# A decoder layer on one core: the first heads' keys and queries as a block pair by seven products, and a fourth such quad in the mixer

## The chip, the core and the metric

The kernel runs on one core of a Trainium2 chip. TensorE multiplies matrices into PSUM banks, VectorE (DVE), ScalarE (ACT) and GpSimd (POOL) work on elements, and the DMA queues move data. Each engine has a queue of its own and takes its instructions in order; semaphores tie the queues together. The metric is the device time of one execution in microseconds (us), lower is better.

## The reference

The layer works on 256 tokens of 2048 features, in float32. One norm feeds one projection, whose columns are queries, keys and values of eight heads and the input of a pooling mixer. Heads and mixer are joined, projected and added to x; then comes a gated feed-forward part with a convolution of width 3.

```python
h = rms_norm(x, attn_norm_g[l])
proj = h @ w_in[l]                       # 2048 x 4096: q, k, v, p of 1024 columns each
q = rms_norm(heads(q), q_norm_g[l]);  k = rms_norm(heads(k), k_norm_g[l])   # per head of 128
a = moba_attention(q, k, heads(v), rel_bias)      # 256 tokens: one causal block
m = multiscale_pool(p, pool_w[l], pool_scale[l])  # windows 2, 4, 8, 16
x = x + jnp.concatenate([a, m], axis=-1) @ w_out[l]
x = x + conv_ffn(rms_norm(x, ffn_norm_g[l]), w_up[l], conv_w[l], conv_b[l], w_down[l])
```

## The kernel before

**Precision.** Every float32 operand of a large product is held as two parts, high and low, in a type that TensorE reads in one pass. A product is three matmuls: high by high, low by high, high by low. Activations are split once. Weights come from memory as float32 and are split on the way: ScalarE copies the high part `wh` (`split_high`, line 142), VectorE subtracts it from the raw weights to get the low part `wl` (`split_low`, line 147).

**Steps.** All weights are one stream of chunks of 128 x 2048, each of two units of 128 x 1024. There are as many steps as units, in the list `steps`; step u is the products of unit u. A half step of plain products is 12 matmuls with 512 columns. The order of the work is written out by hand in the loop at the end of `layer`: in its turn u it emits the high part of unit u + 6, the low part of unit u + 5, the products of unit u, and then whatever `after(u, f)` has hung on that step. So each engine's queue is in the order of this loop. There are four buffers for raw chunks (the next chunk is loaded when one is released), seven for `wh` and six for `wl`.

**Stages before the feed-forward part.** Steps 0 to 15 make the values v of all heads. Steps 16 to 31 make keys and then queries of the first four heads, steps 32 to 47 those of the second four, each as a `tok_block` of eight half steps that accumulates into two PSUM banks, and ends in `head_norm`: ScalarE squares, VectorE reduces, the reciprocal root is taken, VectorE scales. `head_T` turns the result with TensorE; `scores`, `normalise`, `probs_T` and `head_out` are the attention of one head, spread over the steps of the next stage. Steps 48 to 63 are the pooling input. Steps 64 to 81 multiply by the first 1024 columns of the output weights (and by the pooling weights, in between). Steps 82 to 97, the "mixer's block pair", multiply by the other 1024 columns.

**Block pairs and quads.** `down_pair` makes 256 tokens by 1024 columns with four banks, in eight quads (six in the last third of the feed-forward part) of two units. A quad is two feature tiles by two halves of the tokens by two halves of the columns: eight block products, 24 matmuls (`quad`, line 790). Some quads, listed in `MIXED` and `OUT_MIXED`, go by seven products instead (Winograd's form of Strassen's scheme), 21 matmuls (`quad_sums`, line 734). They need sums of blocks of both operands:

- of the weights: `seven_sums` (lines 161 to 163) makes three differences in the raw chunk, and these are split too, into `wh`/`wl` and the tiles `s512` and `s1024`, of which there are two sets (`SECOND` says which quads take the second);
- of the activations: `token_sums` (line 721) makes four sums of 128 tokens on GpSimd, and ScalarE and VectorE split them into `sx` (lines 722, 723).

The first product goes to the bank `aux[0]`, the second to `p5`, the third to `p7`, the fourth to `aux[1]`; three more go straight to the four banks of the pair. `p5` and `p7` are the two small banks, which are also used by the row sums, the scores and the transposes of the probabilities. `add_part` adds `aux`, `p5` and `p7` later.

In the mixer three quads go by seven products (the fourth, sixth and seventh); `mixed_sums` makes their token sums in steps 72 to 77.

**Norm of the input.** The gain is applied to x when it is split, the root mean square later. ScalarE squares x (`square`), GpSimd adds the squares up (`add_squares`, line 357), TensorE sums over partitions and `stats1` (lines 363 to 373), hung on step 18, makes what the heads and the pooling need. The row sum is read from a small bank.

Of the kernel before, what the change touches and what calls it, by code (L numbers as in the profile page):

```python
# [25 lines left out]
F32 = mybir.dt.float32  # L26
# [5 lines left out]
P = 128  # L32
# [28 lines left out]
OUT_MIXED = (3, 5, 6)  # L61
OUT_SECOND = (5,)
# [23 lines left out]
def layer(ctx: ExitStack, tc: tile.TileContext, xT, xtok, wts, par, rel_d, ident_d, icnt_d, out):  # L86
# [261 lines left out]

    def square(a):

        n = min(4 * S, G0 - 4 * a * S)
        nc.scalar.activation(xsq[:, a, :n], xboth[:, 4 * a * S:4 * a * S + n], AF.Square)
        if n < 4 * S:
            nc.scalar.activation(xsq[:, a, n:], xin(0), AF.Square)

    def add_squares(a, b, n):
        nc.gpsimd.tensor_tensor(xsq[:, a, :n], xsq[:, a, :n], b, op=OP.add)

    def stats1():
# [3 lines left out]
        nc.tensor.matmul(ps[:, :S], ones, xsq[:, 0, :S], start=True, stop=True)  # L363
# [19 lines left out]
    def head_norm(ps, name):  # L383
# [11 lines left out]
        n = early.tile([P, NT * 4, HD], F32, name=name, tag="hn")  # L395
# [168 lines left out]
    steps += v_blocks()  # L564
    for b in range(2):
        for nm in ("k", "q"):
            st[nm, b, "end"] = len(steps) + 7
            steps += tok_block(lambda: xh, XT, lambda ps, nm=nm, b=b: st.__setitem__((nm, b), head_norm(ps, nm + "n")))
    for g in (3, 2, 1, 0):
        steps += feat_block(lambda: xh, lambda ps, g=g: pool_window(ps, g))  # L570
        after(len(steps) + (2 if g else 0), lambda g=g: pool_mixed(g))

    assert AHEAD not in PAIRS
    for a, u in enumerate((2, 4, 7, 10)):
        after(u, lambda a=a: square(a))
# [4 lines left out]
    after(10, load_consts)  # L580
    after(18, stats1)
    after(15, load_late)
    after(17, bias_rows)
    after(24, lambda: st.__setitem__(("T", 0), bias_tile(0)))
    for b in range(2):
        for nm, gc in (("k", col(C_KG)), ("q", qs)):
            after(st[nm, b, "end"] + (3 if (nm, b) == ("q", 0) else 2), lambda nm=nm, b=b, gc=gc: st.__setitem__(
                (nm + "T", b), head_T(st[nm, b], gc, nm + "T")))
        at = st["q", b, "end"] + (3 if b else 4)
        for j in range(4):  # L590
            h, u = 4 * b + j, at + 2 * j
# [20 lines left out]

    def open_late():
# [5 lines left out]
        late["sx"] = pool.tile([P, 4, 4, 2, P], F32R, name="sx")  # L619
# [81 lines left out]
    def value(ps, g, j):  # L701
# [7 lines left out]
        if j in late["mixed"]:  # L709
            token_sums(y, j)  # L710

    def token_sums(y, i):
# [3 lines left out]
        sx = late["sx"]  # L716
        s = late["pool"].tile([P, 4, P], F32, name="s", tag="s")
        a11, a21, a12, a22 = y[:, 0, :P], y[:, 0, P:], y[:, 1, :P], y[:, 1, P:]
        for n, (a, b, op) in enumerate(((a21, a22, OP.add), (s[:, 0, :], a11, OP.subtract), (a11, a21, OP.subtract),
                                        (a12, s[:, 1, :], OP.subtract))):  # L720
            nc.gpsimd.tensor_tensor(s[:, n, :], a, b, op=op)  # L721
        nc.scalar.activation(sx[:, i, :, 0, :], s, AF.Copy)
        nc.vector.tensor_tensor(sx[:, i, :, 1, :], s, sx[:, i, :, 0, :].bitcast(F32), op=OP.subtract)

    def mixed_sums(k, i):
# [3 lines left out]
        token_sums(y, i)  # L729
# [6 lines left out]
    def down_pair(bp, nq, final, mixer=False):  # L736
# [4 lines left out]
        order = [2 * k for k in ORDER[nq]]  # L741
        if mixer:
            mixed, second, summed, order = OUT_MIXED, OUT_SECOND, OUT_MIXED, OUT_ORDER
        s_end = 2 * mixed[-1] + 1
        rest = 2 * nq - 1 - s_end

        def hid(k, t):
            act = st["cat"] if mixer else late["hid"]
            return [act[:, k, a, t * P:(t + 1) * P] for a in range(2)]

        def sums(i, n):
            return [late["sx"][:, i, n, a, :] for a in range(2)]
# [118 lines left out]
        for j in range(nq):  # L871
            for h in range(2):
# [12 lines left out]
                for i, n in enumerate((4, 0, 1) if apart else range(5)):  # L885
                    if at == s_end + 1 + (i * (rest - 1) // 5 if end else 0):
                        acts.append(lambda n=n: add_part(n))
# [6 lines left out]
        return runs  # L894

# [11 lines left out]
    steps += down_pair(1, 8, False, True)  # L907
# [58 lines left out]
def chunks(w_in, pool_w, w_out, w_up, w_down):  # L966
# [6 lines left out]

    out = []
    for tiles in V_TILES:
        out.append(np.concatenate([w_in[k * P:(k + 1) * P, 2048 + 512 * b:2560 + 512 * b] for k, b in tiles], axis=1))
    for c0 in (1024, 0, 1536, 512):
# [7 lines left out]

    def halves(w, c0, ks):
        both = []
        for k in ks:
            top, low = (w[i * P:(i + 1) * P, c0:c0 + 1024] for i in (k, k + 1))
# [48 lines left out]
```

## Time and profile before

| | |
|---|---|
| time, median of 3 runs | 1012.52 us (1012.18 to 1013.14) |
| profiled execution, its own time | 1012.62 us |
| span of the profiled execution | 1010.8 us, 13627 instructions |
| TensorE busy (matmul / weight load) | 1006.6 us / 865.0 us |
| VectorE, ScalarE, GpSimd busy | 812.9, 571.4, 92.6 us |
| read from memory | 195.83 MB, 196 GB/s over the span |

The span runs from the first to the last instruction of the profiled execution; its time is 1.8 us more. A busy TensorE means that a matmul was under way. In the groups and timelines a row names the line, the engine, the operation, what it writes and reads, and the shapes; in brackets stands the idle time before it and what ended it. In the chain of waits each row is a stretch of the chain that ended last: start, duration, engine, tile, line and count.

### The profile page before, as it was taken

Reading aid. Unit: us, or ns where it says so; the run is one execution under the profiler, and the core shown is the slowest. Engines: PE = TensorE matmul, PEld = TensorE weight load, DVE = VectorE, ACT = ScalarE, POOL = GpSimd, SP = SyncE. Lnnn points to the kernel's source line nnn. Section 1 sums busy time; section 2 is a strip of 40 time slices with the busy share of each in tenths; the row PEclk is TensorE's granted clock in tenths of the full one; section 3 lists DMA queues with packets and bytes.
Section 4 is the critical chain, followed back from the end, with each engine's and each line's share of the span. In section 5 each row is a group of like instructions: output and inputs, shape, how many; then the busy total and the mean of one; then the engine's idle time right before and its main releaser. Section 6 shows DMA issues by size and latency. Waiting matters only on the chain.

```text
span 1010.8 us, 13627 instructions
## 1 busy us (share of the span) xinstructions
PE 1006.6 (100%) x5250; PEld 865.0 (86%) x5250; DVE 812.9 (80%) x1021; ACT 571.4 (57%) x773; POOL 92.6 (9%) x125
## 2 busy tenths in 40 slices
PE   9999999999999999999999999999999999999998
PEld 8888888888888888888888888888888888888887
DVE  6956666886986888878999678887899977887897
ACT  6744464555565655655566456565555655565572
POOL 0520004601000000000000010000000000000010
PEclk9999999999999999999999999999999999999999
DMA  9784454475453554644676645555357775545474
GB/s 345 275 279 167 167 188 167 168 289 179 166 216 108 187 217 179 240 176 167 231 227 239 220 167 177 214 198 211 140 192 219 290 239 180 191 167 200 175 229 147
DMA packets 32481, 205.49 MB, mean 203 GB/s; under 512 B 3784, under 2 KB 4680, under 8 KB 9632
## 3 DMA queue, kind: packets, MB, share of 16 engines
q1 hardware_dynamic: 29680, 195.84, 52.8%
q0 software_dynamic: 2736, 8.78, 4.3%
q8 instruction: 41, 0.67, 0.3%
q14 instruction: 24, 0.20, 0.1%
HBM read 195.83 MB, written 2.49 MB: 196 GB/s over the span
## 4 chain that ended last, share of the span: by engine, by line
PE 100%; DVE 0%; issue 0%
PE ps_feat L203 35%; PE ps_feat L205 18%; PE ps_down L790 16%; PE ps_tok L190 13%; PE ps_p L734 6%; PE ps_down L734 4%; PE ps_v L197 4%; PE ps_pool L212 1%; PE ps_s L418 1%; PE ps_start L265 0%; PE ps_down L812 0%; PE ps_T L405 0%; PE ps_x2T L651 0%; PE ps_av L451 0%; PE ps_eT L440 0%; PE ps_av L452 0%
## 5 line engine op out<-in xcount | busy, mean ns | idle before, releaser
L203 PE MATMUL ps_feat<-x2h,wh 128*128 128x512 f32 x1408 | 488.9, 392 | 0.0
L147 DVE TENSOR_TENSOR wl<-raw,wh 128x1024 fp32r<-128x1024 f32 x358 | 433.6, 1252 | 42.1 <-ACT wh L142 19.5
L142 ACT ACTIVATE wh<-raw 128x1024 fp32r<-128x1024 f32 x358 | 358.6, 1049 | 104.6 <-DVE raw L161 68.9
L205 PE MATMUL ps_feat<-x2h,wl 128*128 128x256 f32 x1408 | 393.6, 280 | 0.0
L203 PEld LDWEIGHTS ps_feat<-x2h,wh 128*128 128x128 f32 x1408 | 264.3, 188 | 58.2
L205 PEld LDWEIGHTS ps_feat<-x2h,wl 128*128 128x128 f32 x1408 | 264.4, 188 | 0.2
L790 PE MATMUL ps_down<-wh,hid 128*128 128x512 f32 x384 | 94.8, 389 | 0.0
L689 ACT ACTIVATE y<-u,pv 128x256 f32<-128x256 f32 x88 | 48.2, 594 | 77.1 <-DVE u L684 77.1
L790 PEld LDWEIGHTS ps_down<-wh,hid 128*128 128x128 f32 x384 | 72.1, 188 | 15.0
L190 PE MATMUL ps_tok<-wh,xh 128*128 128x512 f32 x256 | 70.1, 396 | 0.0
L690 DVE SCALAR_TENSOR_TENSOR y<-u,pv,y 128x256 f32<-128x256 f32 x88 | 42.4, 482 | 29.5 <-ACT y L689 29.5
L190 PEld LDWEIGHTS ps_tok<-wh,xh 128*128 128x128 f32 x256 | 47.5, 188 | 9.4
L790 PE MATMUL ps_down<-wl,hid 128*128 128x512 f32 x192 | 51.3, 389 | 0.0
L820 POOL DMA_DIRECT2D x<-st x13 | 11.5, 920 | 416.6 <-ACT st L861 282.7
L468 DVE TENSOR_TENSOR fs<-ps_feat,fs 128x512 f32<-128x512 f32 x44 | 30.3, 688 | 21.0 <-ACT fs L467 20.9
L203 PE MATMUL ps_feat<-xh,wh 128*128 128x512 f32 x128 | 46.2, 402 | 0.0
L692 DVE SCALAR_TENSOR_TENSOR y<-u,pv,y 128x256 f32<-128x256 f32 x88 | 42.7, 485 | 3.1
L790 PEld LDWEIGHTS ps_down<-wl,hid 128*128 128x128 f32 x192 | 36.0, 188 | 7.5
L707 ACT ACTIVATE hid<-y 128x512 fp32r<-128x512 f32 x22 | 14.0, 634 | 48.9 <-DVE y L706 48.9
L721 POOL TENSOR_TENSOR s<-y 128x128 f32<-128x128 f32 x22 | 13.7, 624 | 292.7 <-DVE y L706 242.6
L190 PE MATMUL ps_tok<-wl,xh 128*128 128x512 f32 x128 | 39.5, 390 | 0.0
L467 ACT ACTIVATE fs<-ps_feat 128x512 f32<-128x512 f32 x44 | 25.8, 586 | 21.0 <-PE ps_feat L205 20.7
(199 smaller groups left out, 1178.7 us busy)
## 6 DMA issues: line engine op xcount, KB each, us to landing
raw<-in_wts SPq DMA_DIRECT2D x177, 1024.0 KB, 5.0
x<-st POOLq DMA_DIRECT2D x11, 512.0 KB, 10.7
raw<-in_wts SPq DMA_DIRECT2D x4, 512.0 KB, 7.3
x<-in_xtok SPq DMA_DIRECT2D x1, 2048.0 KB, 9.6
raw<-in_wts SPq DMA_DIRECT2D x7, 256.0 KB, 5.5
xboth<-in_xT SPq DMA_DIRECT2D x4, 256.0 KB, 6.1
T<-band POOLq DMA_DIRECT2D x8, 128.0 KB, 7.2
out<-x POOLq DMA_DIRECT2D x2, 512.0 KB, 4.0
```

Source lines behind the costliest of these rows:

```text
L142: nc.scalar.activation(wparts[u][0], raw(u - 1 if u - 1 in seven else u + 1 if u in seven else u), AF.Copy)
L147: nc.vector.tensor_tensor(wl, raw(u - 1 if u - 1 in seven else u + 1 if u in seven else u), wh.bitcast(F32), op=OP.subtract)
L190: nc.tensor.matmul(ps[:, t, :], act[:, k0 + k, a, t * P:(t + 1) * P], w[:, k * 512:(k + 1) * 512], start=(first and k == 0 and n == 0), st ...
L197: nc.tensor.matmul(ps[:, t, :], act[:, k, a, t * P:(t + 1) * P], w[i], start=(first and n == 0), stop=(last and n == 2))
L203: nc.tensor.matmul(ps, wh[:, ws], act[:, k, :, :], start=(first and n == 0), stop=False, skip_group_check=True)
L205: nc.tensor.matmul(ps[:, S:], wl[:, ws], act[:, k, 0, :], start=False, stop=(last and n == len(ks) - 1), skip_group_check=True)
L468: nc.vector.tensor_tensor(dst, ps[:, :, :S], dst, op=OP.add)
L689: nc.scalar.activation(y[:, m, :], u[:, m, 2:], AF.Identity, scale=cw[2], bias=col(C_CB + f))
L690: nc.vector.scalar_tensor_tensor(y[:, m, :], u[:, m, 1:1 + S], cw[1], y[:, m, :], op0=OP.mult, op1=OP.add)
L692: nc.vector.scalar_tensor_tensor(y[:, m, :], u[:, m, :S], cw[0], y[:, m, :], op0=OP.mult, op1=OP.add)
L734: nc.tensor.matmul(ps, act[a], w[i], start=(first and n == 0), stop=(last and n == 2), skip_group_check=skip)
L790: nc.tensor.matmul(bank(t, b), hid(order[j] + h, t)[a], part(w, b if h == 0 else 1 - b)[i], start=(n == 0 and (fresh or mixed[0] == 0 and ...
```

## The change

- **Heads.** Keys and queries of the first four heads become one block pair, `down_pair(0, 8, False, "heads")`, in steps 16 to 31: the left 512 columns are keys, the right 512 queries. The quads at positions 2, 3, 5 and 6 go by seven products (steps 20 to 23 and 26 to 29); the second and the last of these take the second set of tiles. `head_sums` adds the two parts of x, makes the four token sums on VectorE in steps 16, 18, 20 and 22, and `sums_split` splits them two steps later each. One of the pair's two bank pairs comes from `aux`, and its bank pair `ps_p` from the accumulators. `head_parts` (step 30) and `heads_end` (step 31) put the result together in SBUF. `head_norm` of the keys follows at step 31, of the queries at step 32.
- **Attention of the first heads.** The keys are turned at step 34, the queries at step 36; the scores start at step 37 instead of 35. The second keys are turned at step 43 instead of 41.
- **Mixer.** A fourth quad, the third, goes by seven products. Token sums are made on VectorE in steps 70 to 76 and split one step later each. In the feed-forward part they stay on GpSimd.
- **Squares.** They are added on VectorE in steps 5, 8 and 11, the last sum into a tile of its own, `xsum`. `stats1` stays at step 18.
- **Smaller moves.** `bias_rows` goes from step 17 to 24, the first bias tile from 24 to 28, the second from 42 to 44. The weights are laid out for the pair on the host.

```diff
-OUT_MIXED = (3, 5, 6)
-OUT_SECOND = (5,)
+OUT_MIXED = (2, 3, 5, 6)
+OUT_SECOND = (3, 6)
+HEADS_MIXED = (2, 3, 5, 6)
+HEADS_SECOND = (3, 6)
...
     def add_squares(a, b, n):
-        nc.gpsimd.tensor_tensor(xsq[:, a, :n], xsq[:, a, :n], b, op=OP.add)
+        nc.vector.tensor_tensor(xsq[:, a, :n], xsq[:, a, :n], b, op=OP.add)
...
-        nc.tensor.matmul(ps[:, :S], ones, xsq[:, 0, :S], start=True, stop=True)
+        nc.tensor.matmul(ps[:, :S], ones, xsum, start=True, stop=True)
...
+    def open_heads():
+        hs = keep.tile([P, 3 + len(HEADS_MIXED), 1024], F32R, name="hs", tag="c")
+        late["s"] = [seven_tiles(early, 0), [[hs[:, 0, :512], hs[:, 0, 512:]], [hs[:, 1, :], hs[:, 2, :]]]]
+        late["sx"] = [hs[:, 3 + i, :].rearrange("p (n a t) -> p n a t", n=4, a=2)
+                      for i in range(len(HEADS_MIXED))]
...
+    def token_sums(y):
+        eng = nc.gpsimd if "mixed" in late else nc.vector
+        s = late["sums"] = (late["pool"].tile([P, 4, P], F32, name="s", tag="s") if "pool" in late else
+                            early.tile([P, 4, P], F32, name="s", tag="hn"))
         a11, a21, a12, a22 = y[:, 0, :P], y[:, 0, P:], y[:, 1, :P], y[:, 1, P:]
         for n, (a, b, op) in enumerate(((a21, a22, OP.add), (s[:, 0, :], a11, OP.subtract), (a11, a21, OP.subtract),
                                         (a12, s[:, 1, :], OP.subtract))):
-            nc.gpsimd.tensor_tensor(s[:, n, :], a, b, op=op)
-        nc.scalar.activation(sx[:, i, :, 0, :], s, AF.Copy)
-        nc.vector.tensor_tensor(sx[:, i, :, 1, :], s, sx[:, i, :, 0, :].bitcast(F32), op=OP.subtract)
-
-    def mixed_sums(k, i):
+            eng.tensor_tensor(s[:, n, :], a, b, op=op)
+
+    def sums_split(i):
+        sx, s = late["sx"], late["sums"]
+        nc.scalar.activation(sx[i][:, :, 0, :], s, AF.Copy)
+        nc.vector.tensor_tensor(sx[i][:, :, 1, :], s, sx[i][:, :, 0, :].bitcast(F32), op=OP.subtract)
+
+    def head_sums(k):
+        y = early.tile([P, 2, S], F32, name="y", tag="sq")
+        nc.vector.tensor_tensor(y, xh.bitcast(F32)[:, k:k + 2, 0, :], xh.bitcast(F32)[:, k:k + 2, 1, :], op=OP.add)
+        token_sums(y)
...
         def banks():
-            box["tok"] = [acc("ps_down") for t in range(NT)]
+            box["tok"] = [(aux if heads and t == 0 else acc)("ps_down") for t in range(NT)]
...
-                box["aux"], box["p5"], box["p7"] = aux("ps_p"), small("ps_p5"), small("ps_p7")
+                box["aux"], box["p5"], box["p7"] = (acc if heads else aux)("ps_p"), small("ps_p5"), small("ps_p7")
...
+        def head_parts(n):
+            pa_, p5, p7 = box["aux"], box["p5"], box["p7"]
+            if n == 0:
+                box["raw"] = k, q = [early.tile([P, NT, 512], F32, name=t + "raw", tag=t + "T") for t in "kq"]
+                nc.scalar.activation(k[:, 0, :], pa_[:, 0, :], AF.Copy)
+                nc.vector.tensor_tensor(q[:, 0, :], pa_[:, 1, :], k[:, 0, :], op=OP.add)
+                nc.vector.tensor_tensor(k[:, 1, :], p7, q[:, 0, :], op=OP.add)
+            elif n == 1:
+                k, q = box["raw"]
+                nc.vector.tensor_tensor(q[:, 1, :], p5, k[:, 1, :], op=OP.add)
+                nc.vector.tensor_tensor(q[:, 0, :], p5, q[:, 0, :], op=OP.add)
+
+        def heads_end():
+            for b, raw_ in enumerate(box["raw"]):
+                for t in range(NT):
+                    nc.vector.tensor_tensor(raw_[:, t, :], bank(t, b), raw_[:, t, :], op=OP.add)
+            st["k", 0], st["qraw"] = head_norm(box["raw"][0], "kn"), box["raw"][1]
...
+    steps += v_blocks()
+    h0 = len(steps)
+    after(12, open_heads)
+    st["k", 0, "end"] = st["q", 0, "end"] = h0 + 15
+    for i, j in enumerate(HEADS_MIXED):
+        after(h0 + 2 * i + 2, lambda i=i: sums_split(i))
+        after(h0 + 2 * i, lambda j=j: head_sums(2 * j))
+    steps += down_pair(0, 8, False, "heads")
...
-    after(4, lambda: add_squares(0, xsq[:, 1, :], 4 * S))
-    after(7, lambda: add_squares(0, xsq[:, 2, :], 4 * S))
-    after(10, lambda: (add_squares(0, xsq[:, 3, :], 4 * S), add_squares(0, xsq[:, 0, 2 * S:], 2 * S),
-                       add_squares(0, xsq[:, 0, S:2 * S], S)))
+    after(5, lambda: add_squares(0, xsq[:, 1, :], 4 * S))
+    after(8, lambda: add_squares(0, xsq[:, 2, :], 4 * S))
+    after(11, lambda: (add_squares(0, xsq[:, 3, :], 4 * S), add_squares(0, xsq[:, 0, 2 * S:], 2 * S),
+                       nc.vector.tensor_tensor(xsum, xsq[:, 0, :S], xsq[:, 0, S:2 * S], op=OP.add)))
...
     after(18, stats1)
...
-    after(17, bias_rows)
-    after(24, lambda: st.__setitem__(("T", 0), bias_tile(0)))
+    after(24, bias_rows)
+    after(28, lambda: st.__setitem__(("T", 0), bias_tile(0)))
...
-        at = st["q", b, "end"] + (3 if b else 4)
+        at = st["q", b, "end"] + (3 if b else 6)
+        if b == 0:
+            after(at - 5, lambda: st.__setitem__(("q", 0), head_norm(st["qraw"], "qn", keep, "c")))
...
-        after(o0 + 8 + 2 * i, lambda i=i, j=j: mixed_sums(OUT_ORDER[j], i))
+        after(o0 + 6 + 2 * i, lambda j=j: mixed_sums(OUT_ORDER[j]))
+        after(o0 + 7 + 2 * i, lambda i=i: sums_split(i))
```

More of the change, by code (lines that the diff above doesn't have):

```diff
@@ L347, in layer @@
     rrow = keep.tile([P, S], F32, name="rrow", tag="rrow")
+    xsum = early.tile([P, S], F32, name="xsum")
     def square(a):
@@ L394, in head_norm @@
         rsqrt(r, m, NT * 4, early, "h")
[L395 removed]
+        n = pool.tile([P, NT * 4, HD], F32, name=name, tag=tag)
         nc.vector.tensor_tensor(n, psv, r[:, :, None].to_broadcast([P, NT * 4, HD]), op=OP.mult)
@@ L618, in open_late @@
         nc.sync.dma_start(late["x2"], xtok)
-        late["sx"] = pool.tile([P, 4, 4, 2, P], F32R, name="sx")
+        sx = pool.tile([P, 4, 4, 2, P], F32R, name="sx")
+        late["sx"] = [sx[:, i] for i in range(4)]
         late["s"] = [seven_tiles(pool, 0), None]
@@ L741, in down_pair @@
         order = [2 * k for k in ORDER[nq]]
+        mixer, heads = kind == "mixer", kind == "heads"
         if mixer:
             mixed, second, summed, order = OUT_MIXED, OUT_SECOND, OUT_MIXED, OUT_ORDER
+        if heads:
+            mixed, second, summed, order = HEADS_MIXED, HEADS_SECOND, HEADS_MIXED, XT
         s_end = 2 * mixed[-1] + 1
@@ L747, in hid @@
         def hid(k, t):
-            act = st["cat"] if mixer else late["hid"]
+            act = xh if heads else st["cat"] if mixer else late["hid"]
             return [act[:, k, a, t * P:(t + 1) * P] for a in range(2)]
         def sums(i, n):
-            return [late["sx"][:, i, n, a, :] for a in range(2)]
+            return [late["sx"][i][:, n, a, :] for a in range(2)]
         def bank(t, b):
@@ L884, in down_pair @@
                 acts = [run]
-                for i, n in enumerate((4, 0, 1) if apart else range(5)):
+                for i, n in enumerate(range(2) if heads else (4, 0, 1) if apart else range(5)):
                     if at == s_end + 1 + (i * (rest - 1) // 5 if end else 0):
-                        acts.append(lambda n=n: add_part(n))
+                        acts.append(lambda n=n: (head_parts if heads else add_part)(n))
                         run.adds = not end
@@ L904, in layer @@
     for i, j in enumerate(OUT_MIXED):
-        after(o0 + 8 + 2 * i, lambda i=i, j=j: mixed_sums(OUT_ORDER[j], i))
+        after(o0 + 6 + 2 * i, lambda j=j: mixed_sums(OUT_ORDER[j]))
+        after(o0 + 7 + 2 * i, lambda i=i: sums_split(i))
     after(len(steps) - 1, lambda: open_temps(True))
-    steps += down_pair(1, 8, False, True)
+    steps += down_pair(1, 8, False, "mixer")
     f0 = len(steps)
@@ L972, in feat, with halves @@
         return [w[k * P:(k + 4) * P, c0:c0 + 256].reshape(4, P, 256).transpose(1, 0, 2).reshape(P, HALF) for k in ks]
+    def halves(w, c0, ks):
+        both = []
+        for k in ks:
+            top, low = (w[i * P:(i + 1) * P, c0:c0 + 1024] for i in (k, k + 1))
+            both += [top, np.concatenate([low[:, 512:], low[:, :512]], axis=1)]
+        return both
     out = []
@@ L976, in chunks @@
         out.append(np.concatenate([w_in[k * P:(k + 1) * P, 2048 + 512 * b:2560 + 512 * b] for k, b in tiles], axis=1))
-    for c0 in (1024, 0, 1536, 512):
+    out += halves(np.concatenate([w_in[:, 1024:1536], w_in[:, :512]], axis=1), 0, range(0, KT, 2))
+    for c0 in (1536, 512):
         out += tok(w_in, c0, range(0, KT, 2))
@@ L984, in chunks @@
     out += tok(w_out, 512, OK)
[L986 to L989, printed above, removed]
-            both += [top, np.concatenate([low[:, 512:], low[:, :512]], axis=1)]
-        return both
     out += halves(w_out, 1024, OUT_ORDER)
```

66 lines of the change are left out of this document (33 added, 33 removed).

## The prediction

> **What bounds the kernel now.** First comes the page: how busy each engine is, the granted clock and the chain that ended last.
>
> ```profile
> PE 1006.6 (100%) x5250; PEld 865.0 (86%) x5250; DVE 812.9 (80%) x1021; ACT 571.4 (57%) x773; POOL 92.6 (9%) x125
> ...
> PEclk9999999999999999999999999999999999999999
> ...
> PE 100%; DVE 0%; issue 0%
> ```
>
> TensorE is busy through the whole span at the full clock, and the chain is TensorE alone. Second, the view of who waited for whom, for TensorE, has one row:
>
> ```profile
> PE ps_start L265 <- DVE ones L262: 1.1, 1, 1.1
> ```
>
> So after its start TensorE waits for nobody. A product taken away is worth its full duration, and a wait put in costs its full duration, because nothing later can catch it up. Third, the chain in order of time prices the products (start, duration, what):
>
> ```profile
> 49.06 8.16 PE ps_tok L190 x36
> 57.22 0.43 PE ps_row L363 x2
> 264.55 2.72 PE ps_p L734 x12
> 267.27 2.04 PE ps_down L734 x9
> 269.31 5.44 PE ps_down L790 x24
> ```
>
> A matmul of 512 columns takes 8.16/36 = 0.227 us. A half step is 12 of them, 2.72; a quad is 24, 5.44; a quad by seven products is 12 + 9, 4.76.
>
> Fourth, VectorE where four of eight quads go by seven products today, by stages (span, then busy time of PE, PEld, DVE, ACT, POOL):
>
> ```profile
> 510.00:552.00 42.00, 42.00 (x187) 34.79 (x186) 41.24 (x41) 24.99 (x28) 1.83 (x2) 1.00 0.74 250
> ```
>
> There VectorE works 41.24 of 42 us. Two rows show how closely it serves TensorE: the low part of a combination of weights, and the matmul group that first reads this tile.
>
> ```profile
> 511.75 1.22 DVE L175 TENSOR_TENSOR s1024l<-raw,s1024h 128x1024 fp32r<-128x1024 f32 x1
> 513.79 0.62 PE L734 MATMUL ps_p<-s1024h,sx 128*128 128x512 f32 x2
> ```
>
> The tile is ready 0.8 us before its group starts. So four quads of eight fill VectorE, and that stage makes no token sums of its own. The question is whether the first heads' pair, where the sums come on top, still fits.
>
> **What is removed.** The heads' pair has four quads by seven, each 3 products shorter: 4 x 0.68 = 2.72 us. The mixer goes from three to four: 0.68. Together 3.40 us of TensorE, everything else equal.
>
> **What a quad by seven costs VectorE.** One quad of the mixer, from its first low part to the next unit's:
>
> ```profile
> 268.74 1.22 DVE L147 TENSOR_TENSOR wl<-raw,wh 128x1024 fp32r<-128x1024 f32 x1
> 269.87 0.68 DVE L168 TENSOR_TENSOR s512l<-raw,s512h 128x512 fp32r<-128x512 f32 x1
> 270.59 1.22 DVE L161 TENSOR_TENSOR raw<-raw 128x1024 f32<-128x1024 f32 x1
> 271.85 0.69 DVE L162 TENSOR_TENSOR raw<-raw 128x512 f32<-128x512 f32 x1
> 272.57 0.69 DVE L163 TENSOR_TENSOR raw<-raw 128x512 f32<-128x512 f32 x1
> 273.18 1.22 DVE L147 TENSOR_TENSOR wl<-raw,wh 128x1024 fp32r<-128x1024 f32 x1
> 274.47 1.23 DVE L175 TENSOR_TENSOR s1024l<-raw,s1024h 128x1024 fp32r<-128x1024 f32 x1
> 275.62 4.62 DVE L147 TENSOR_TENSOR wl<-raw,wh 128x1024 fp32r<-128x1024 f32 x4
> ```
>
> The first unit takes 273.18 - 268.74 = 4.44, the second 2.44: 6.88 us, against 4.76 of TensorE. The last row prices a plain unit: 4.62/4, about 1.14 back to back.
>
> **What the token sums add.** They lie beside the mixer today:
>
> ```profile
> 221.37 0.69 DVE L728 TENSOR_TENSOR fs<-cat 128x512 f32<-128x512 f32 x1
> 224.68 0.69 DVE L723 TENSOR_TENSOR sx<-s,sx 128x512 fp32r<-128x512 f32 x1 [2.62 <-ACT sx L722]
> 126.52 0.42 DVE L457 TENSOR_TENSOR cat<-ps_av,cat 128x256 fp32r<-128x256 f32 x1 [1.14 <-ACT cat L456]
> 222.14 0.46 POOL L721 TENSOR_TENSOR s<-fs 128x128 f32<-128x128 f32 x1 [14.74 <-DVE fs L728]
> 58.81 0.17 DVE L371 TENSOR_SCALAR e<-t 128x2 f32<-128x2 f32 x1
> ```
>
> No VectorE sum of 128 columns is in the trace. From 512 columns (0.69) and 256 (0.42) the line goes to 0.29 at 128, which I take; the bounds are 0.17 (two columns) and 0.46 (what GpSimd needs). One set of sums is 0.72 + 4 x 0.29 = 1.88, its low half 0.69 more. Four sets in the heads' pair are 10.3 us. In the mixer VectorE stands 2.62 us per set today, waiting for GpSimd and ScalarE; after the change that wait is gone, as the split comes a step later. There 4 x 2.57 = 10.3 replaces 3 x (0.69 + 2.62 + 0.69) = 12.0 us. After quad 3 it waits for TensorE:
>
> ```profile
> 261.92 1.22 DVE L147 TENSOR_TENSOR wl<-raw,wh 128x1024 fp32r<-128x1024 f32 x1 [1.48 <-PE ps_down L790]
> ```
>
> A fourth quad, 6.88 - 2.28 = 4.6 us, fits: at quad 6 the last tile is ready by 275.62 and first read three triples into the quad, at 269.31 + 5.44 + 4.76 + 2.04 = 281.55; the added quad takes at most 4.6 + 0.68 of these 5.9 us. So I count the mixer's 0.68 in full.
>
> **The squares.** GpSimd's sums cost VectorE time while they run:
>
> ```profile
> 28.03 2.67 POOL L357 TENSOR_TENSOR xboth<-xboth 128x1024 f32<-128x1024 f32 x1 [27.05 <-ACT xboth L352]
> 28.93 2.85 DVE L147 TENSOR_TENSOR wl<-raw,wh 128x1024 fp32r<-128x1024 f32 x1 [0.50 <-ACT wh L142]
> ```
>
> A 1.22 us subtraction takes 2.85 beside one. On VectorE the sums are 3 x 1.23 + 0.69 + 0.42 = 4.8 us in steps 5 to 11, and the stretching goes. I cost this at nothing: VectorE still comes to step 15 ahead of its free tile. If that cover were gone, the start below would move by up to 4.8.
>
> **VectorE's queue through the heads' pair.** It works in the order of the program. The start is set by the low parts' six buffers: unit 20's needs unit 14's. The rule shows here, where the subtraction for unit 23 starts as unit 17 ends:
>
> ```profile
> 54.34 1.07 PE L190 MATMUL ps_tok<-wh,xh 128*128 128x512 f32 x4
> 54.59 1.22 DVE L147 TENSOR_TENSOR wl<-raw,wh 128x1024 fp32r<-128x1024 f32 x1 [1.49 <-PE ps_tok L190]
> 57.69 0.42 DVE L341 TENSOR_SCALAR trow<-ps_row 128x256 f32<-128x256 f32 x1 [1.87 <-PE ps_row L363]
> 61.30 3.49 DVE L147 TENSOR_TENSOR wl<-raw,wh 128x1024 fp32r<-128x1024 f32 x3
> ```
>
> The statistics of the first norm take 57.69 to 61.30, 3.61 us, of which the first operation (0.42) frees the row sum's bank. ScalarE must meanwhile empty two v tiles:
>
> ```profile
> 46.38 1.03 ACT L381 ACTIVATE v<-ps_v 128x1024 f32<-128x1024 f32 x1 [2.11 <-PE ps_v L197]
> ```
>
> Each evacuation delays a copy for which a subtraction of quad 2 waits. I take 1.0 us for both; the bounds are 0 and 2.06.
>
> Unit 14 ends at 49.06 - 2.72 = 46.34, so VectorE starts quad 2 (units 20, 21) at 46.4.
> - VectorE: 6.88 + 1.0 for quad 2's weights: 54.3. Its sums, 1.88: 56.2. Quad 3's weights, 6.88: 63.1. Low half of quad 2's sums: 63.8. Quad 3's sums: 65.7. Row statistics: 66.1 for the bank, 69.3 in all.
> - TensorE reaches quad 2 at 49.06 + 4 x 2.72 + 0.43 = 60.37. The second matmul of its second triple needs the low half of the sums at 61.28 and gets it at 63.8: 2.5 us. The third triple takes the small bank of the row sum and waits from 64.25 to 66.1: 1.85. Quad 2 ends at 69.5.
> - VectorE: plain unit 24 and the low half for quad 3: 71.1. TensorE wanted it at 70.4: 0.7. Quad 3 ends at 74.95, plain quad 4 at 80.4.
> - VectorE: quad 5's sums 73.0, unit 25 74.1, unit 26 78.6, low half 79.3, quad 6's sums 81.15, unit 27's low part 82.3, quad 5's last tile 83.6, quad 6's weights 90.5, its low half 91.2, and 0.2 for ScalarE's copy before it: 91.4.
> - TensorE wants unit 27's low part at 81.5 (0.8 us late; quad 5 ends at 85.95) and quad 6's sums at 86.85: 4.55.
>
> The waits are 4.35 + 0.7 + 0.8 + 4.55 = 10.4 us. As a cross-check, with no wait the last is due at 60.37 + 4.76 + 4.76 + 5.44 + 4.76 + 0.91 = 81.0, and VectorE comes at 91.4. Queued behind these instructions are the low parts of units 30 to 35, which still come in time.
>
> **The tail of the pair.** Quad 7 ends at 100.7. VectorE has five low parts, four partial sums of 0.70, one low part and four last sums: 103.85. Then come the norms, priced by today's:
>
> ```profile
> 93.99 1.02 ACT L387 ACTIVATE sq<-ps_tok 128x1024 f32<-128x1024 f32 x1 [2.11 <-PE ps_tok L190]
> 95.05 1.22 DVE L389 TENSOR_REDUCE m<-sq 128x8 f32<-128x1024 f32 x1 [2.50 <-ACT sq L387]
> 99.00 4.62 DVE L147 TENSOR_TENSOR wl<-raw,wh 128x1024 fp32r<-128x1024 f32 x4
> ```
>
> A square is 1.02 and VectorE's share 99.00 - 95.05 = 3.95. The keys are ready at 108.8, their transposes come after unit 34, at 108.9; the queries at 115.1, wanted at 115.2. These are ties; I take 0.4 us in all, with 0 and 2 as bounds. The attention steps then run two steps later beside the second heads' plain units, where VectorE had rests of 1.5 us a unit (row at 54.59): nothing.
>
> **The sum.** 1012.62 (the profiled execution; its span is 1010.8, and it lies 0.1 above the median 1012.52) - 2.72 - 0.68 + 10.4 + 0.4 = 1020.0 us. Of the bounds, sixteen small sums give -1.9 or +2.7, ScalarE's waits -1.0 or +1.1, the tail -0.4 or +1.6. They will not all fall together; its own range is 1016.5 to 1023.5.
>
> **Rivals.**
> - **VectorE keeps up, 1009.2.** The place is the low half of quad 2's sums. If VectorE is there by 61.3, clears the row sum by 61.7 and reaches quad 6's sums by 81.0, nothing waits, and the whole 3.40 is gained. For it: five units' lead (13.6 us), and the full VectorE of 510 to 552. Against: that lead is where the count already starts, and sums and statistics add 10.3 + 3.6 us.
> - **Only the first half waits, 1014.3.** Quad 4 gives VectorE 5.44 us for 2.28 of weights. Were the rest quicker by 5.4, only 4.35 + 0.7 would be lost: 1012.62 - 3.40 + 5.05. Against: quads 5 and 6 with two sets of sums come right behind.
> - **The gaps lower the clock, 1024.3.** The clock row is 9 throughout, and no gap in the trace is longer than 1.1 us; the two waits here are above 4 each. If each were followed by as long a stretch at half the clock, it would lose half of 4.35 and of 4.55 more, 4.4 (an estimate). The Trainium skill, in TensorE: Matmul & The Clock Gate, part The HAM clock gate, has this rule: after an idle window of about 3.4 us the clock goes to half, until a busy window has passed. No run here shows it yet, and the gaps may be too broken for it.
> - **The second keys wait for the pair's banks, 1022.9.** Should their accumulator get the bank that the last sums read, TensorE stands for 4 x 0.70 + 0.1. Against:
>
> ```profile
> 119.03 2.75 PE ps_tok L190 x12
> 122.28 1.23 DVE L396 TENSOR_TENSOR kn<-ps_tok,hr 128x1024 f32<-128x1024 f32 x1
> ```
>
> The second queries start at 119.03 while the second keys' tile, two allocations earlier, is read until 123.5: the bank released longest ago is handed out, here the earlier freed one.
>
> **Chances.** Forecast 0.62, kept up 0.13, first half 0.11, clock 0.07, banks 0.07. The range 1012.5 to 1023.5 holds the forecast, the first half, the banks and a little of the clock, about 0.8. 0.2% is 2 us, about what a measurement can tell from no change. Faster is the first rival and a little beside it, 0.14; the same, a part of the first half, 0.05; slower 0.81.
>
> **What would show it.** TensorE waits at the second and third triple of quad 2 for VectorE (the low half of sx, the mean of the row), little at quads 3 and 5, over 4 us at quad 6; VectorE without rest from 46 to 104 us; the mixer pair 0.68 shorter without a wait. A TensorE with no row of waits there, or a VectorE sum of 128 columns far from 0.29, would make this wrong.

## The result and the profile after

The changed kernel takes 1021.31 us in the median (1020.64 to 1021.55), the kernel before, run alongside, 1012.83; the ratio is 1.0083, with a 95% interval of 1.0071 to 1.0095. It is slower by 8.5 us; 1020.0 was forecast. The profiled execution took 1021.55 us, with a span of 1019.7.

The page, with the lines that answer to those of before:

```profile
span 1019.7 us, 13670 instructions
...
PE 1009.4 (99%) x5235; PEld 865.3 (85%) x5235; DVE 849.7 (83%) x1101; ACT 581.2 (57%) x789; POOL 75.8 (7%) x108
...
PEclk9989999999999999999999999999999999999999
```

TensorE has 15 matmuls fewer and is busy 2.8 us longer, because the third slice of the clock row is an 8: some matmuls ran slowly. Who waited for whom, for TensorE:

```profile
PE ps_p L719 <- ACT hs L702: 4.1, 2, 2.3
PE ps_p L719 <- DVE trow L343: 1.3, 1, 1.3
PE ps_start L267 <- DVE ones L264: 1.1, 1, 1.1
PE ps_p L719 <- DVE hs L703: 0.5, 2, 0.2
```

Where the kernel before had only the row of its start, three new ones add up to 5.9 us, all in the seven-product matmuls (L719). The timeline of TensorE shows where (start, duration, and in brackets the idle time before, with what ended it):

```profile
63.41 0.49 PE L719 MATMUL ps_p<-wh,hs 128*128 128x512 f32 x1 [1.81 <-ACT hs L702]
64.14 0.50 PE L719 MATMUL ps_p<-wh,hs 128*128 128x512 f32 x1 [0.23 <-DVE hs L703]
...
66.13 1.22 PE L719 MATMUL ps_p<-wh,hs 128*128 128x512 f32 x2 [1.25 <-DVE trow L343]
...
90.34 0.50 PE L719 MATMUL ps_p<-wh,hs 128*128 128x512 f32 x1 [2.33 <-ACT hs L702]
91.06 0.50 PE L719 MATMUL ps_p<-wh,hs 128*128 128x512 f32 x1 [0.23 <-DVE hs L703]
```

These are quad 2 (its sums, then the bank of the row sum) and quad 6 (its sums). VectorE at the same places, and its waits from 49 to 100 us:

```profile
46.95 1.23 DVE L149 TENSOR_TENSOR wl<-raw,wh 128x1024 fp32r<-128x1024 f32 x1 [1.10 <-issue]
...
63.40 0.69 DVE L703 TENSOR_TENSOR hs<-s,hs 128x512 fp32r<-128x512 f32 x1 [0.24 <-ACT hs L702]
...
65.66 0.42 DVE L343 TENSOR_SCALAR trow<-ps_row 128x256 f32<-128x256 f32 x1
...
90.32 0.69 DVE L703 TENSOR_TENSOR hs<-s,hs 128x512 fp32r<-128x512 f32 x1 [0.24 <-ACT hs L702]
```

```profile
DVE hs L703 <- ACT hs L702: 0.7, 3, 0.3
DVE s1024l L177 <- ACT s1024h L168: 0.5, 1, 0.5
DVE rs_s L338 <- ACT rs_r L337: 0.3, 1, 0.3
DVE s512l L170 <- ACT s512h L168: 0.3, 1, 0.3
```

From 46.95 to 91.01 us VectorE rests for under 2 us in all. TensorE's rows name ScalarE (L702), but VectorE's low half of the same sums ends only 0.7 us after ScalarE's high half, so the name alone does not tell whose queue is late; experiments 2 and 3 do.

The waits are only half of it. The stages of TensorE (span, busy, clock in the third number from the right) show slow stretches behind both gaps:

```profile
64.00:66.00 2.00, 0.73 (x2) 0.30 (x2) 1.93 (x7) 0.00 (x0) 0.00 (x0) 0.69 0.92 217
66.00:68.00 2.00, 1.87 (x4) 1.49 (x5) 1.40 (x10) 1.15 (x5) 0.00 (x0) 0.50 0.88 313
68.00:70.00 2.00, 2.00 (x6) 1.60 (x5) 1.92 (x4) 2.00 (x3) 0.00 (x0) 0.50 0.07 29
70.00:72.00 2.00, 2.00 (x7) 1.53 (x7) 1.97 (x4) 0.91 (x2) 0.00 (x0) 0.60 0.00 0
...
92.00:94.00 2.00, 2.00 (x7) 1.57 (x6) 2.00 (x3) 2.00 (x4) 0.00 (x0) 0.52 0.92 385
94.00:96.00 2.00, 2.00 (x8) 1.54 (x7) 2.00 (x3) 1.57 (x4) 0.00 (x0) 0.63 0.87 291
```

At half the clock a matmul takes some 0.43 us instead of 0.227. The 15 from 66.13 to 72.20 took 6.1 us instead of 3.4, the 15 from 91.63 to 96.65 took 5.0 instead of 3.4.

The mixer is as counted; its chain after the change:

```profile
268.32 2.72 PE ps_p L719 x12
271.04 2.04 PE ps_down L719 x9
273.08 2.72 PE ps_p L719 x12
275.80 2.04 PE ps_down L719 x9
277.84 5.44 PE ps_down L778 x24
```

The first two of its four quads follow without a gap. Over the whole of the mixer the lag behind the kernel before falls from 9.2 to 8.5 us, the 0.68 of one quad.

### The profile page after: what moved, and what is told of

Same layout as the page of the kernel before. It is cut to its first block, busy times and chain, and to the rows that moved or that the text cites. A ratio compares the mean times of both kernels' runs of the same rounds, so it can differ in the third digit from the quotient of the medians.

```text
span 1019.7 us, 13670 instructions
## 1 busy us (share of the span) xinstructions
PE 1009.4 (99%) x5235; PEld 865.3 (85%) x5235; DVE 849.7 (83%) x1101; ACT 581.2 (57%) x789; POOL 75.8 (7%) x108
## 4 chain that ended last, share of the span: by engine, by line
PE 94%; DVE 4%; ACT 1%; issue 1%; POOL 0%; ACTq 0%; POOLq 0%; DVEq 0%
PE ps_feat L205 33%; PE ps_feat L207 17%; PE ps_down L778 15%; PE ps_tok L192 9%; PE ps_p L719 6%; PE ps_down L719 5%; PE ps_v L199 4%; DVE wl L149 1%; PE ps_pool L214 1%; PE ps_s L422 1%; DVE raw L163 0%; ACT wh L144 0%; PE ps_start L267 0%; PE ps_down L800 0%; DVE s L698 0%
## 5 line engine op out<-in xcount | busy, mean ns | idle before, releaser
L149 DVE TENSOR_TENSOR wl<-raw,wh 128x1024 fp32r<-128x1024 f32 x358 | 428.4, 1237 | 27.4 <-ACT wh L144 17.8
L207 PE MATMUL ps_feat<-xh,wl 128*128 128x256 f32 x128 | 35.8, 280 | 0.0
L192 PE MATMUL ps_tok<-wh,xh 128*128 128x512 f32 x128 | 35.6, 400 | 0.0
L199 PE MATMUL ps_v<-wh,xh 128*128 128x512 f32 x128 | 35.2, 397 | 0.0
```

The lines of the kernel that those rows point to most:

```text
L149: nc.vector.tensor_tensor(wl, raw(u - 1 if u - 1 in seven else u + 1 if u in seven else u), wh.bitcast(F32), op=OP.subtract)
L192: nc.tensor.matmul(ps[:, t, :], act[:, k0 + k, a, t * P:(t + 1) * P], w[:, k * 512:(k + 1) * 512], start=(first and k == 0 and n == 0), st ...
L199: nc.tensor.matmul(ps[:, t, :], act[:, k, a, t * P:(t + 1) * P], w[i], start=(first and n == 0), stop=(last and n == 2))
L207: nc.tensor.matmul(ps[:, S:], wl[:, ws], act[:, k, 0, :], start=False, stop=(last and n == len(ks) - 1), skip_group_check=True)
```

## The experiments

Two theories stand against each other. **VectorE**: its queue is too long for the heads' pair, as the prediction counts it. **ScalarE**: its copies of the sums (L702) stand too late in its own queue, which is what TensorE's rows name. A third question is what the slow clock costs and whether the gaps cause it.

### 1. The mixer's part alone

```diff
 (the kernel before)
-OUT_MIXED = (3, 5, 6)
-OUT_SECOND = (5,)
+OUT_MIXED = (2, 3, 5, 6)
+OUT_SECOND = (3, 6)
...
-            nc.gpsimd.tensor_tensor(s[:, n, :], a, b, op=op)
+            eng.tensor_tensor(s[:, n, :], a, b, op=op)       # VectorE in the mixer
...
+        after(o0 + 6 + 2 * i, lambda j=j: mixed_sums(OUT_ORDER[j]))
+        after(o0 + 7 + 2 * i, lambda i=i: sums_split(i))
```

> The kernel before with the mixer's part of the change alone: the fourth quad by seven products, token sums on VectorE in steps 70 to 76, split one step later. If the heads' pair is the cause of the loss, the mixer is 0.68 us shorter here and TensorE waits nowhere: 1012.1 us, that is 0.7 below the kernel before, and the chain shows 4 x 2.72 + 4 x 2.04 in the mixer with no wait in between. If the mixer's fourth quad costs VectorE too much as well, TensorE shows waits between the mixer's quads or at the first feed-forward steps, and the time is 1012.8 or more.

Measured: 1012.12 us against 1012.73; the ratio is 0.9994, with an interval of 0.9984 to 1.0004. The runs alone can't tell this from no change, but the trace has no wait of TensorE beyond its start, and the transposes behind the mixer come at 289.11 instead of 289.72, 0.61 earlier. The loss is not in the mixer; the rows of waits of the changed kernel put it in the heads' pair.

### 2. Token sums of the heads made once

```diff
-        after(h0 + 2 * i, lambda j=j: head_sums(2 * j))
+        if i == 0:
+            after(h0, lambda j=j: head_sums(2 * j))
```

> The changed kernel, but the token sums of the heads are made once, for the first of the four quads, and the other three split these same sums again: VectorE does 3 x 1.85 = 5.6 us less in the heads' pair, ScalarE has the same work in the same order. What is left out: the token sums of three quads. Theory VectorE (its queue is too long): the low half for the last quad comes at 91.0 - 5.6 = 85.4 instead of 91.0, the wait for the row sum's bank goes, the wait before quad 6 shrinks to 0 to 2 us: 1013 to 1016 us, about 1014.5. Theory ScalarE (its copies of the sums stand too late in its own queue): only the wait for the bank goes, 1019 to 1020 us.

Measured: 1014.30 us, ratio 1.0014 (1.0005 to 1.0024). The kernel leaves out the token sums of three quads. Only VectorE's work was cut, ScalarE's queue kept every copy in its order, and 7.0 of the 8.5 us are gone. TensorE's waits:

```profile
PE ps_p L719 <- ACT hs L702: 2.6, 2, 1.8
PE ps_start L267 <- DVE ones L264: 1.1, 1, 1.1
PE ps_p L719 <- DVE hs L703: 0.8, 3, 0.3
```

The row for the bank (`trow`) is gone, and before quad 6 only 1.0 us is left, within the 0 to 2 expected. The waits at quad 2 (1.80 and 0.23) stay, as its sums are made as before. The clock stayed at 1.00 in this profiled execution; in the other nine its mean over the span is 0.998 or 0.999, and they took 1014.20 to 1014.77 us instead of 1013.86.

### 3. The split in the step that makes the sums

```diff
-        after(h0 + 2 * i + 2, lambda i=i: sums_split(i))
         after(h0 + 2 * i, lambda j=j: head_sums(2 * j))
+        after(h0 + 2 * i, lambda i=i: sums_split(i))
```

> The changed kernel, but each set of sums of the heads is split in the step that makes it, not two steps later. ScalarE's copy then stands ahead of the weight copies. Theory ScalarE: the waits that TensorE's rows name after ScalarE (4.1 us in two places) and the slow stretches behind them go, 1012 to 1016 us. Theory VectorE: its queue holds the same work and 4 x 0.4 us more of waiting for the copy, and the last thing needed becomes the weights of quad 6 instead of its sums, so the waits move to other rows and the time stays near 1021, 1020 to 1022.

Measured: 1020.64 us, ratio 1.0077 (1.0062 to 1.0092). All rows that named ScalarE's copy of the sums are gone, and the time is the same as that of the change within 0.7 us (two waits of 0.3 us are left out here):

```profile
PE ps_p L719 <- DVE trow L343: 5.8, 1, 5.8
PE ps_start L267 <- DVE ones L264: 1.1, 1, 1.1
PE ps_p L719 <- DVE wl L149: 0.7, 1, 0.7
```

The waits moved to whatever VectorE reaches last: the bank of the row sum in quad 2, a weight's low part in quad 6. ScalarE's place in the rows was the last link of VectorE's chain. This theory falls.

### 4. The statistics taken out of the stretch

```diff
         mean_sq(t, ps[:, :S])
+        st["trow"] = t
+
+    def stats1b():
+        t = st["trow"]
...
-    after(18, stats1)
+    after(13, stats1)
+    after(24, stats1b)
```

> The changed kernel, but the first norm's statistics are taken out of the stretch: the row sum and its mean come at step 13, the other 3.2 us at step 24, behind the last quad's low half. VectorE has 3.6 us less to do before the last deadline (87.4 instead of 91.0), and the bank of the row sum is free early. Theory VectorE: no wait for the bank, the first wait for the sums still there, a shorter wait at quad 6: 1016 to 1017.5 us. Theory ScalarE: only the wait for the bank goes (1.25 us and what it slows), 1018.5 to 1020.

Measured: 1019.45 us, ratio 1.0064 (1.0049 to 1.0079): 1.9 us less than the change, where 4 to 5 were expected. The waits:

```profile
PE ps_p L723 <- ACT hs L706: 3.9, 2, 2.3
PE ps_start L267 <- DVE ones L264: 1.1, 1, 1.1
PE ps_T L413 <- DVE kn L404: 1.0, 1, 1.0
PE ps_T L413 <- ACT kT L415: 0.6, 1, 0.6
PE ps_row L367 <- DVE xsum L930: 0.3, 1, 0.3
```

The bank's wait is gone, and the last low half ends at 88.30 instead of 91.01, 2.7 us earlier instead of 3.6: at step 13 TensorE had to wait 0.3 us for the sum of squares and do the row sum (0.43), so the whole pair began later. And the 3.2 us that went to step 24 came back as waits of 1.0 and 0.6 us for the keys' norm and for its copy, which had been ties. The expectation left out these two. The time lies within what the ScalarE theory gave (1018.5 to 1020) and outside what the VectorE theory gave, so this run does not speak for VectorE; experiments 2 and 3 separate the two.

### 5 and 11. The gaps filled with matmuls by zeros

```diff
+    zero = early.tile([P, P], F32R, name="zero")
+    nc.vector.tensor_scalar(zero, ones, 0.0, None, op0=OP.mult)
...
+                rest_ = xh[:, 0:1, :, :].rearrange("p k a t -> p (k a t)")
+                if heads and j in (2, 6):
+                    for n in range(8 if j == 2 else 28):    # 18 in experiment 11
+                        nc.tensor.matmul(box["aux"][:, 0, :], zero, rest_, start=first and n == 0, stop=False)
-                triple(box["aux"][:, 0, :], hid(k, 0), s1, first, last)
+                triple(box["aux"][:, 0, :], hid(k, 0), s1, first and not heads, last)
                 triple(box["p5"], sums(i, 0), part(t13, 0), first, last)
+                if heads and j == 2:
+                    for n in range(5):
+                        nc.tensor.matmul(box["p5"], zero, rest_, start=False, stop=False)
```

> The changed kernel with matmuls by a tile of zeros put in where TensorE waits: 8 before quad 2's first triple, 5 behind its second, 28 before quad 6's first (41 x 0.227 = 9.3 us); they add zero, nothing is left out. They fill waits, so they cost nothing as long as VectorE sets the pace. Theory clock (the slow stretches come from the gaps): the granted clock stays at 1.00 from 60 to 98 us, quad 2's slow stretch is taken back by longer waits before quad 6 (VectorE still comes at 91.0), and only the slow stretch behind quad 6 is won: 1019 to 1020 us. Theory other cause of the slow clock: the stretches at 0.5 to 0.6 stay, 1021 us or more.

Measured with 28: 1021.23 us, ratio 1.0083 (1.0065 to 1.0101), no gain. The clock did what was expected; the stretch from 60 to 98 us, which had 0.87 in the changed kernel, reads

```profile
60.00:98.00 38.00, 37.00 (x158) 29.08 (x158) 36.05 (x59) 20.63 (x28) 2.22 (x4) 1.00 0.54 178
```

But VectorE had the last sums ready at 90.54, and the 28 matmuls ran to 91.9, the sums being read only after another triple's worth: some 2 us of filler too many, which ate what the clock gave. Hence experiment 11, with 18.

> As e5, but with 18 matmuls by zeros before quad 6 instead of 28. In e5 the 28 ran 2.3 us beyond the point where VectorE had the sums ready. With 18 they end before it, VectorE sets the pace to the end, and the clock stays at 1.00: 2 us below the changed kernel, 1019.0 to 1019.6. If the slow stretches cost nothing, 1021.

Measured: 1019.77 us, ratio 1.0069 (1.0054 to 1.0085), 1.5 us less than the changed kernel, a little less than the 2 expected. The clock reads 1.00 here too:

```profile
60.00:98.00 38.00, 36.94 (x157) 28.73 (x156) 36.05 (x59) 20.64 (x28) 2.21 (x4) 1.00 0.54 176
```

So the gaps lower the clock, and this costs about 1.5 us of the 8.5. VectorE is busy 36.05 us in these 38 with the clock full, as it was 36.06 with the clock halved: it sets the pace either way. What quad 2's slow stretch takes, the wait before quad 6 gives back: in experiment 11 TensorE reaches quad 6 at 85.67, in the changed kernel at 87.17, and both then have to stay there until VectorE is ready.

### 6. Small sums by GpSimd

```diff
-        eng = nc.gpsimd if "mixed" in late else nc.vector
+        eng = nc.vector if "pool" in late and "mixed" not in late else nc.gpsimd
```

> The changed kernel, but the 16 small sums of the heads' token sums are made by GpSimd (the sum of the two parts of x stays on VectorE). VectorE is rid of 16 x 0.29 = 4.6 us, GpSimd gets 16 x 0.46 = 7.4. If GpSimd slows VectorE as in the row of before where a subtraction of 1.22 took 2.85 beside 2.67 us of GpSimd (0.6 us lost for each of GpSimd's), VectorE loses 4.5 and nothing is won: 1020 to 1022 us. If small sums do not disturb, the last deadline is met 4.6 us earlier: 1015 to 1017.

Measured: 1019.62 us, ratio 1.0067 (1.0049 to 1.0085). It lies between the two expectations: GpSimd does disturb, but not as much as the row of before had it. On GpSimd, first beside a VectorE subtraction of weights, then beside short operations:

```profile
54.79 1.37 POOL L698 TENSOR_TENSOR s<-y 128x128 f32<-128x128 f32 x1 [53.81 <-DVE y L707]
...
63.88 0.46 POOL L698 TENSOR_TENSOR s<-y 128x128 f32<-128x128 f32 x1 [4.58 <-DVE y L707]
```

and on VectorE the subtraction of raw weights beside them, 1.23 us in the changed kernel, and the low half of the last sums:

```profile
56.74 1.37 DVE L163 TENSOR_TENSOR raw<-raw 128x1024 f32<-128x1024 f32 x1
...
88.13 0.69 DVE L703 TENSOR_TENSOR hs<-s,hs 128x512 fp32r<-128x512 f32 x1 [0.21 <-ACT hs L702]
```

This low half ends 2.2 us earlier than in the changed kernel, 0.6 of it because VectorE began the pair at 46.36 instead of 46.95. So 1.6 of the 4.6 us came through. The GpSimd sums took two to three times as long beside long VectorE operations (0.79 to 1.44 us instead of 0.46), and those of VectorE that were stretched lost 0.14 to 0.26 us. The Trainium skill (SBUF — State Buffer, SBUF: two separate sides) says that a VectorE instruction with two SBUF inputs and a GpSimd instruction that reads SBUF take turns whole, the later one standing still. The GpSimd sum of 1.37 us, which starts 0.17 us into a subtraction of 1.22, agrees with that; VectorE's own loss is less than one whole GpSimd sum, and what it consists of is not shown.

### 7 and 8. Two and three quads

```diff
-HEADS_MIXED = (2, 3, 5, 6)
-HEADS_SECOND = (3, 6)
+HEADS_MIXED = (3, 6)          # experiment 8: (2, 4, 6)
+HEADS_SECOND = (6,)           # experiment 8: (4,)
...
-        after(h0 + 2 * i + 2, lambda i=i: sums_split(i))
-        after(h0 + 2 * i, lambda j=j: head_sums(2 * j))
+        after(h0 + 2 * j - 2, lambda i=i: sums_split(i))
+        after(h0 + 2 * j - 4, lambda j=j: head_sums(2 * j))
```

Each set of sums is made four steps before its quad begins and split two steps before.

> The changed kernel with two quads by seven products in the heads' pair (the fourth and the seventh) instead of four, sums four and split two steps ahead of... their quad's first step less two. VectorE has 2 x (4.6 + 2.5) = 14.2 us less work, which is more than the 10 us by which it was late. Theory VectorE: no wait before the quads and the clock at 1.00, a gain of 2 x 0.68 + 0.68 = 2.04 us on the kernel before: 1010.6 to 1011.2. If the block pair itself (its banks, the later norms) costs time, it stays above 1012.

> The same with three quads (the third, fifth and seventh). Theory VectorE: 7.1 us less than four quads, so it is late by some 3 us, in one or two waits of under 3 us; 2.72 us are saved: 1012 to 1015 us, about 1013.5. So two, three and four quads are not in a line: 1010.8, 1013.5, 1021.

Measured: two quads 1011.51 us, ratio 0.9987 (0.9977 to 0.9996), one wait of 0.2; three quads 1014.03, ratio 1.0013 (1.0003 to 1.0022), with one wait:

```profile
73.95 0.50 PE L719 MATMUL ps_p<-wh,hs 128*128 128x512 f32 x1 [1.84 <-DVE hs L703]
```

Behind it the clock reads 0.82 from 72 to 76 us and 0.75 from 76 to 80. Two, three and four quads take 1011.5, 1014.0 and 1021.3: the saving is 0.68 each, the price begins where VectorE's queue is full. (Which quads they are, and when their sums are made, changes along with the number.) Two quads fall short of the expected 1010.6 to 1011.2 by 0.3.

### 9 and 10. Three quads with a lighter VectorE

Both have three quads (the third, fifth and seventh), the split in the step that makes the sums, the wide half of the first norm's root at step 38, and the first heads' transposes and scores one step later. In experiment 9 ScalarE also makes the sum of the two parts of x, from x and its gain:

```diff
-        rsqrt(rrow, t, S, early, "w")
+        after_row.append(lambda: rsqrt(rrow, t, S, early, "w"))
...
+    def head_y(i, k):                                   # experiment 9 only
+        y = early.tile([P, 2, S], F32, name=f"y{i}", tag=("sq", "kT", "qT")[i])
+        for c in range(2):
+            nc.scalar.activation(y[:, c, :], xin(k + c), AF.Copy, scale=gain(k + c))
+        st["y", i] = y
...
+        after(12 + i, lambda i=i, j=j: head_y(i, 2 * j))
+        after(h0 + 2 * j - 4, lambda i=i: head_sums(i))
+        after(h0 + 2 * j - 4, lambda i=i: sums_split(i))
+    after(14, open_heads)
...
+    after(38, lambda: after_row.pop()())
```

> Three quads by seven products (third, fifth, seventh), with VectorE's queue relieved of what can go elsewhere: the sum of the two parts of x is taken from x and the gain by ScalarE in steps 12 to 14, the wide half of the first norm's root (1.3 us) goes to step 38, each set of sums is split in the step that makes it, and the transposes and scores of the first heads come one step later. By the count of VectorE's queue the last quad's tiles come about 1 us before they are needed, and the queue is not late anywhere: no wait, clock 1.00, 2.04 + 0.68 = 2.72 us below the kernel before: 1010.1, 1009.8 to 1010.8. If three quads are too many all the same, a wait of 1 to 2 us and a slow stretch appear: 1012 to 1014.

> As e9, but VectorE makes the sum of the two parts of x, 3 x 0.72 = 2.1 us more. By the same count it is late by 1.1 to 1.4 us at the last quad's weights, in a gap too short to lower the clock: 1011.3, 1010.6 to 1012.5. So the 2.1 us on VectorE cost 1 to 1.4 us in e10 and nothing in e9.

Measured: experiment 9 takes 1010.63 us, ratio 0.9979 (0.9970 to 0.9988), experiment 10 1011.69, ratio 0.9989 (0.9980 to 0.9998). In experiment 9 TensorE waits for nothing but its start. The last tile for quad 6, on VectorE, and its first reader on TensorE:

```profile
80.89 1.22 DVE L177 TENSOR_TENSOR s1024l<-raw,s1024h 128x1024 fp32r<-128x1024 f32 x1
```

```profile
83.11 0.39 PE L724 MATMUL ps_p<-s1024l,hs 128*128 128x512 f32 x1
```

It is ready 1.0 us early, as counted. In experiment 10 one wait of 0.5 us is left, for a low part of quad 6's weights, where 1.1 to 1.4 were counted; its time is within its range. Experiment 9 is faster than the kernel before by 2.2 us and than the change by 10.7. Of the 2.72 us it should save, 2.35 are there at the transposes behind the mixer (287.37 instead of 289.72); the other 0.37 is lost ahead of them, behind the heads' pair's start, at a place that was not looked for.

## Why the prediction was right

- **VectorE's queue.** This is the step on which the forecast stood, and it held nearly to the tenth: quad 2's low half forecast at 63.8, measured at 64.1; the row sum's bank at 66.1, measured at 66.1; quad 6's low half at 91.4, measured at 91.0. VectorE's 128-column sum was taken as 0.29 us and is 0.28 to 0.29. That the places fit to the tenth is in part luck: VectorE started 0.5 us later than taken, as unit 14 ended later, and its queue from there to the last low half was 44.1 us long, where 45.0 were counted. The term that was too large is the set of sums: 1.65 us in the queue instead of 1.88, as the small ones start 0.2 us apart, though each lasts 0.28. Experiments 2, 3, 7 and 8 show that this queue is the cause.
- **The waits.** Forecast were 4.35 us at quad 2, 0.7, 0.8 and 4.55; the rows show 3.3, nothing, nothing and 2.6. At quad 2 TensorE came 0.4 us later than counted, and the single matmuls around the gaps took 0.40 to 0.50 us instead of 0.227. From there on the difference is the clock: TensorE ran at half speed and so came later to the places where it would have waited. Up to the last wait this does not change the sum, as VectorE sets the pace.
- **The clock.** It was put as a rival of its own, with 0.07 and 4.4 us. That step was wrong in two ways. It happens together with the forecast, not instead of it: both gaps lowered the clock. And it costs about 1.5 us (experiment 11), because a slow stretch ahead of the next wait is free; only the one behind quad 6 is paid. The forecast of 1020.0 lacks 1.3 us to 1021.3: the 1.5 us of the clock and the late start of 0.5 were not in it; the sums, counted 0.9 us too long, and the tail of 0.4, which was not paid, work the other way. So that the total came as near as it did is in part luck too. The bound of "above 4 each" for the gaps was too high as well: they are 1.81 + 0.23 + 1.25 and 2.33 + 0.23, with matmuls in between.
- **The rule of the skill.** The Trainium skill (TensorE: Matmul & The Clock Gate, The HAM clock gate) has the clock fall after an idle window of about 3.4 us. The trace agrees that gaps halve the clock, and that this lasts 3.41 us or twice that, but no whole window had to be idle: 1.84 us in experiment 8 did it. The measurement decides; the last section has the line between the gaps that did it and those that did not.
- **The rival "VectorE keeps up"** fell at the place where it was to be decided: the low half of quad 2's sums came at 64.1 instead of 61.3. **"Only the first half waits"** fell at quad 6. **The banks**: the second keys began without a wait, as the row of before had it.
- **The tail** was taken as 0.4 us; no wait is in the rows. It was a tie indeed: in experiment 4, 3.2 us more on VectorE gave waits of 1.0 and 0.6 there.
- **The mixer** saved 0.68 and waited for nothing, in the changed kernel and alone (experiment 1). **The squares** cost nothing: VectorE stood idle 1.10 us ahead of unit 20, and experiments 7 and 9, which keep them on VectorE, are faster than the kernel before.

The sum in the trace, up to the transposes behind the mixer (298.25 after, 289.72 before, 8.5 us): a start at 0.5 us later, the pair's 2.72 saved, 11.4 lost in the pair (5.85 of waits, the rest, nearly 5.6, slow matmuls and restarts), 0.68 saved in the mixer.

## What to carry to other kernels

Where TensorE is the bound, count what a scheme with fewer products asks of the engine that prepares its operands, over the stretch between the first buffer that engine can have and the last deadline: here 6.9 us of VectorE for a quad's weights, where plain ones take 2.3, and another 2.3 for its sums, for 0.68 us of TensorE. The gain is linear in the number of quads, and the price begins only where that engine's queue no longer fits in the stretch. So a smaller dose (three quads, with 2.1 us moved to ScalarE and 1.3 us of the norm moved out of the stretch) won where four lost. The engine that a wait's row names can be the last link of another engine's chain; taking work from each in turn tells them apart.

## What was not expected of the hardware

- **Gaps of about 2 us lower TensorE's clock, though not every one; where they fall decides.** Each trace keeps a record of the clock granted to TensorE. From its first entry to the end of the kernel's work it knows only 1.0 and 0.5, and it changes only at whole multiples of 3.41 us from that entry: in the changed kernel the clock is half from 64.76 to 71.59 us (two such windows) and from 92.07 to 95.48 (one), with six windows in between. Count TensorE's idle time window by window in all thirteen traces. These are all the windows at full clock with more than 1.1 us idle (the ends of matmuls are modelled, so the hundredths are rough):

| run | window, us | idle in it, us | clock after it |
|---|---|---|---|
| experiment 6 | 59.36 to 62.78 | 1.45 | 1.0 |
| experiment 2 | 58.81 to 62.23 | 1.58 | 1.0 |
| experiment 3 | 59.81 to 63.22 | 1.65 | 1.0 |
| experiment 4 | 84.85 to 88.26 | 1.65 | 1.0 |
| experiment 8 | 71.18 to 74.59 | 1.86 | 0.5 |
| the change, quad 6 | 88.65 to 92.07 | 1.91 | 0.5 |
| the change, quad 2 | 61.35 to 64.76 | 2.04 | 0.5 |
| experiment 6 | 83.26 to 86.67 | 2.21 | 0.5 |
| experiment 4 | 60.96 to 64.37 | 2.33 | 0.5 |
| experiment 3 | 63.22 to 66.63 | 3.41 | 0.5 |

So in these traces the clock halves behind a window that was idle for 1.86 us or more, and not behind one that was idle for 1.65 or less; single matmuls in between did not help. A window at half the clock with 0.71 us or more idle was followed by a second one, a window without idle time by the full clock. The gap of 1.80 us in experiment 2 ran over the end of its window and had no effect; the one of 1.84 in experiment 8 lay in one window and had.

The first entry comes 4.20 to 6.88 us after the start, in another place in every trace. So the same kernel should go either way, and the single executions agree: of the ten of experiment 8, three have a mean clock of 1.000 over the span and took 1013.46 to 1013.62 us; the other seven have 0.998 or 0.999 (one window at half the clock makes 0.998) and took 1013.76 to 1014.89. No run moved a gap within its window on purpose, so this line is read from the gaps that happened to be there.

- **Matmuls by zeros hold the clock up.** In experiments 5 and 11 it stayed at 1.00 through the same stretch.
- **The first matmuls differ from trace to trace.** The first four of the values took, in the kernel before and in the changed kernel:

```profile
4.92 1.51 PE L197 MATMUL ps_v<-wh,xh 128*128 128x512 f32 x4
```

```profile
4.92 2.00 PE L199 MATMUL ps_v<-wh,xh 128*128 128x512 f32 x4
```

They start at the same time and in the same order; this is the 0.5 us by which the changed kernel was late before the pair. The record of the clock shows why: its first entry, at full clock, is at 5.66 us in the kernel before and at 6.74 in the changed one. Ahead of it a matmul follows the last one after 0.427 us, behind it after 0.227. In the other profiles these four take 1.17 to 2.05 us, by and large the longer the later that entry is. The Trainium skill (TensorE: Matmul & The Clock Gate, The HAM clock gate) has the point at which the clock rises after a start vary from run to run, with a window that runs free of the kernel; these rows agree, and the multiples of 3.41 us in each record are that window.
